# Zero rows under the remainders of the keys in the first attention of a two-block kernel

## The chip, the cores and the metric

The kernel runs on one core of one Trainium2 chip, as one launch. Its time is the device time of that launch in microseconds, the median of several runs; lower is better. Engines are named as in the profile: PE is TensorE's matmul, PEld its weight load, DVE is VectorE, ACT is ScalarE, POOL is GpSimd, SP issues the DMAs.

## The reference, cut to what matters

The reference takes 256 tokens of width 1024 through a first block (gated branch mixer, cross attention to a memory, mixture of experts) and a second one: an attention with three branches (`nsa_mixer`), an MLP, a differential attention and another MLP, each under a modulation that depends on a condition. What counts here is the attention with three branches: 16 query heads of width 64 in four groups, each group with its own key and value head for a "selected" and a "window" branch.

```
q_rot = apply_partial_rope(rms_norm(q), cos, sin)          # 16 heads x 64
ks    = apply_partial_rope(rms_norm(ks, k_gain[1]), ...)   # 4 groups x 64, selected
kw    = apply_partial_rope(rms_norm(kw, k_gain[2]), ...)   # 4 groups x 64, window
ss = einsum('bghqd,bgqnld->bghqnl', q_rot, ks_selected) / 8   # causal softmax, then times values
sw = einsum('bghqd,bgkd->bghqk',   q_rot, kw_window)   / 8    # causal softmax, then times values
out = gate0 * o_cmp + gate1 * o_sel + gate2 * o_win
```

With 256 tokens there are four blocks of 64 keys and the four best are selected, so both branches see all earlier keys: the scores of a query are the products with two key sets under one causal mask.

## The kernel before, in words

A scheduler sets the order of the instructions of each engine before the run, from the program and a simulated timeline; on the chip each engine takes its instructions in that fixed order and waits on semaphores.

[...] To keep the precision, an operand is kept as two tiles: its rounded value (hi) and the remainder (lo). For the scores, `qrT` holds the rotated queries of a head with the hi part in rows 0 to 63 and the lo part in rows 64 to 127, [128, 256 tokens] a head. `kTd` holds the hi part of the keys twice over the rows, so that one product over 128 rows gives (hi + lo of q) times hi of k. `kTl` holds the lo part of the keys in 64 rows only; a second product, over the 64 rows of the queries' hi part, adds hi of q times lo of k to the same PSUM bank. A third product of the identity (`identb`) with the causal mask `cmask` adds the mask.

`kv_block(s, c0)` makes keys and values of one branch s: a projection, the norm of the heads, the rotation, transposes on TensorE, then `kTd` by ScalarE (line 1189) and `kTl` by VectorE (line 1190). The layout is [rows, group, token tile, branch, 128 keys], so one product takes both branches of a token tile.

`att(p_, t)` does two heads (pair `p_`) and one tile of 128 queries (`t`). For t = 0 a product has 256 columns, for t = 1 it has 512. Line 1393 holds the products with `kTd` and `kTl`, line 1396 those with the mask. VectorE takes the maximum (lines 1400 and 1401), ScalarE the exponential with its sum (line 1411), VectorE divides and gates (1413 to 1417). Two rounds later TensorE transposes the probabilities (line 1428), ScalarE or VectorE copies them out (1434, 1432), and a round later TensorE multiplies with the values (line 1444) and adds the compressed branch (line 1446). `skewed` runs 16 such generators (eight pairs, two tiles each) as a software pipeline, one new one each round. Between rounds, `fill` puts modulation products: `ada_step` loads 512 KB of `w_ada` into one of two buffers (line 427) and multiplies it with the condition (line 432, eight products with 32 columns of stationary each).

The score products take four PSUM banks in turn, two for each `att`.

On GpSimd, `rescale` multiplies the residual stream `xT` with gains (line 1136) and with a norm (line 1137) near 534 to 557 us; the tiles `Sc` are cleared at line 1350 for the compressed branch.

Of the kernel before, what the change touches and what calls it, by code (L numbers as in the profile page):

```python
# [11 lines left out]
F32 = mybir.dt.float32  # L12
F32R = mybir.dt.float32r
# [3 lines left out]
OP = mybir.AluOpType  # L17
# [21 lines left out]
def two_blocks_kernel(ctx, tc, A, out):  # L39
# [10 lines left out]
    # PSUM's eight banks, shared out anew for each phase: outputs of long runs of matmuls (mm), what hangs  # L50
    # on a chain of other engines (ax), long accumulations (acc), modulation rows (ada)
# [24 lines left out]
    # ---------------------------------------------------------------- helpers  # L76
# [6 lines left out]
    def behind(e, ins):  # L83
        """ins is issued behind the fence of its engine (an order for the scheduler, no wait)"""
        if e in fence:
            tc.add_manual_dep(ins.ins, fence[e].ins.name, NOSYNC, reason="behind the norm")
        return ins
# [17 lines left out]
    class wmat:  # L105
        """the hi and lo parts of w2d[:, c0:c0+cols], as [128, cols] pairs, one for each 128 rows"""
# [30 lines left out]
    def mm_fm(ps, w, x, xk, c, first, last, ncol=P, **kw):  # L137
        """ps[ncol features, tokens] += w[:, c:c+ncol]^T x[:, xk, :]"""
        (whi, wlo), (xh, xl) = w, x
        T.matmul(ps, whi[:, c:c + ncol], xh[:, xk, :], start=first, stop=False, **kw)  # L140
        T.matmul(ps, whi[:, c:c + ncol], xl[:, xk, :], start=False, stop=False, **kw)  # L141
        return T.matmul(ps, wlo[:, c:c + ncol], xh[:, xk, :], start=False, stop=last, **kw)  # L142

    def mm_tm(ps, xT, xk, t0, w, first, last):
        """ps[128 tokens, cols] += x[:, xk, t0:t0+128]^T w"""
# [5 lines left out]
    def fm_block(w2d, K, c0, x, w=None, first=False):  # L151
        """256 output features: a bank [128, 2, tokens]; first: x is still under way"""
        w = w.load() if w else wmat(w2d, K, c0, 256)
        ps = bank("fm")
        if first:
            # one group for the bank: its first product clears both halves
# [11 lines left out]
    def tm_steps(w2d, c0, xT, emit, cols=512, w=None):  # L168
        """512 output columns for both token tiles, a tile at a time"""
# [19 lines left out]
    def later(gen):  # L189
        """gen's first step now, its other steps one at a time behind the next blocks of matmuls"""  # L190
# [12 lines left out]
    def skewed(gens, fill=None):  # L203
        """software pipeline: each round starts a generator and moves the others on by one step, newest first"""
# [13 lines left out]
    def log_exp():  # L218
        """ScalarE's table with both Ln and Exp, for what follows"""
# [5 lines left out]
    def inv_rms(ss, n, scale, tag, pool=None):  # L225
        """1/sqrt(ss * scale + EPS) for ss [128, n], with one Newton step on top of the tables' exp(-ln / 2)"""
# [5 lines left out]
    def newton(ss, y, h, t, scale, add=EPS, p=P):  # L232
        """y = 1/sqrt(ss * scale + add)"""
# [7 lines left out]
    def norm_rows(x, dst):  # L241
        """dst = x / rms(x), for x [128 tokens, 1024]"""
# [20 lines left out]
    def rstd(ss, add=EPS):  # L263
        """1/rms of the tokens from their sums of squares on all partitions"""
# [4 lines left out]
    class norm:  # L269
        """the norm of x times gA plus gB, as hi and lo"""  # L270
# [6 lines left out]
        def squares(self, c):  # L277
            """features 256c on of x: their squares' sums over partitions; those of the first 768 are added up before"""
# [39 lines left out]
    def resid(c, ps, gate=None, nx=None):  # L318
        """features 256c on: x += gate * ps, and what the next norm takes from them"""
# [11 lines left out]
    def to_fm(h, aT, t, g):  # L331
        """rows [128 tokens, 1024] times gains to hi/lo feature-major columns of token tile t"""
# [12 lines left out]
    def out_first(aT, w, k1, k0=0, ps=None):  # L345
        """the first block of out_proj up to row block k1, for an input that is still under way"""
# [7 lines left out]
    def out_proj(aT, w2d, nx, gate=None, ws=(), ps0=None):  # L354
        """x += gate * (a @ w)"""
# [9 lines left out]
    # ---------------------------------------------------------------- constants  # L365
# [10 lines left out]
    # the residual stream, feature-major  # L376
# [7 lines left out]
    # causal mask of a diagonal block, twice  # L384
# [6 lines left out]
    # ---------------------------------------------------------------- adaLN rows  # L391
# [3 lines left out]
    def cols(n, name, *parts):  # L395
        """vectors as columns: rows of 128 values turned, [128, n]"""
# [14 lines left out]
    # a part of a layer's modulation row at a time, 1024 columns, in steps of 128 rows of w_ada: on TensorE, 256 for  # L411
    # each of its four column tiles, or summed up over steps on VectorE
# [22 lines left out]
    def ada_mm(n=1, pool=None):  # L435
        """steps on TensorE, or with a pool for the sum on VectorE"""
# [47 lines left out]
    def adaln(i, j, g):  # L484
        """columns of (1 + scale) * g and shift of sublayer j"""
# [10 lines left out]
    # ================================================================ block 1  # L496
    with tc.tile_pool(name="kv", bufs=1, reuse_waits="tile") as kvp:
# [15 lines left out]
        # ---- gated branch mixer  # L513
        win = A["w_in"][0]
        log_exp()
        with tc.tile_pool(name="mix", bufs=1, reuse_waits="tile") as mx:
# [17 lines left out]
            def turned(src, name, c):  # L534
                """features 256c on of two tiles of rows, feature-major"""
# [18 lines left out]
            # the memory's norm, for its keys and values  # L554
# [10 lines left out]
            # rope tables, [128 tokens, tile, 8]  # L565
# [48 lines left out]
            # conv branch  # L614
# [30 lines left out]
            # gated short conv branch  # L645
# [20 lines left out]
            # pool branch  # L666
# [20 lines left out]
            # layer norm over the conv channels  # L687
# [29 lines left out]
            # gates 1 and 2 with their branches  # L717
# [43 lines left out]
        # ---- cross attention  # L761
        phase(mm=3, ax=3, ss=1)
        with tc.tile_pool(name="xa", bufs=2, reuse_waits="tile") as xp, tc.tile_pool(name="ad", bufs=B_X, reuse_waits="tile") as ad:
# [68 lines left out]
            # logits, feature-major, then turned  # L832
# [11 lines left out]
    # ---- hierarchical mixture of experts  # L844
# [7 lines left out]
    def head_rstd(pool, src, n, dim, tag):  # L852
        """1/rms over the last axis of src [128, n, dim]"""
# [6 lines left out]
    def head_norm(pool, dst, src, n, gain, tag):  # L860
        """dst [128, n, 64] = rms_norm(src) * gain, for src in PSUM"""
# [4 lines left out]
    def rope(pool, dst, src, t, n):  # L866
        """the first 16 of 64 columns of dst [128, n, 64] rotated; dst may be src"""
# [11 lines left out]
    with (tc.tile_pool(name="ad3", bufs=5, reuse_waits="tile") as ad,  # L879
# [18 lines left out]
        def first_max(l, nm):  # L898
            """max over the last axis, and the one-hot of its first place"""
# [11 lines left out]
        # ranks within the groups  # L911
# [21 lines left out]
        # the tokens' rows, for the gather  # L933
# [16 lines left out]
        def gating():  # L950
            """o1: each token's weights of the experts of its group"""
# [35 lines left out]
        # the first weights, in tiles of their own  # L987
# [5 lines left out]
        def moe_pass(slot, okm, nx=None, pre=()):  # L993
            """experts on the tokens whose slot is set, 128 slots to a group"""
# [102 lines left out]
        # tokens past a group's 128 slots: a pass of their own, before the others'  # L1097
# [9 lines left out]
        # block 1 ends in x r1 g_f with r1 = 1/sqrt(mean(x^2) + EPS); the mean square of that and its EPS over  # L1107
        # r1^2 are mean(x^2 (g_f^2 + EPS)) + EPS^2, so that block 2 starts on x g_f over the root of that
# [31 lines left out]
    # ================================================================ block 2  # L1140
    # ---- NSA
# [9 lines left out]
    with ExitStack() as st2:  # L1151
# [4 lines left out]
        if True:  # L1156
# [6 lines left out]
            # keys twice over the rows, and what their rounding leaves  # L1163
            kTd = npl.tile([P, 4, 2, 2, P], F32R, name="kTd")
            kTl = npl.tile([64, 4, 2, 2, P], F32R, name="kTl")
            vTM = npl.tile([P, 2, 2, 4, 64], F32, name="vTM")
            qT = act.tile([P, 8, S], F32, tag="aTl", name="qT")
            # rotated queries, a head's hi over its lo
# [5 lines left out]
            # selected and window keys and values  # L1174
            def kv_block(s, c0):
                def emit_k(t, ps):
# [13 lines left out]
                    V.tensor_tensor(kTl[:, :, t, s, :], z[0:64], kTd[0:64, :, t, s, :].bitcast(F32), op=OP.subtract)  # L1190
# [3 lines left out]
            # queries  # L1194
# [22 lines left out]
            def gate_block():  # L1217
                """sigmoid of the gates' logits: feature-major products, then turned"""
# [14 lines left out]
            # compressed keys and values: token-pair columns of four groups, then the position embeddings  # L1233
            if True:
# [23 lines left out]
                def compress():  # L1258
# [27 lines left out]
                    # keys: [64 (group, n), 64]  # L1286
# [21 lines left out]
                    # values: [(4 copies, 32 n), group, 64]  # L1308
# [26 lines left out]
            # compressed branch: probabilities times gate, transposed to [(4 heads, 32 n), tile of heads, q]  # L1335
# [366 lines left out]
```

## Time and profile before

| | us |
|---|---|
| median of 3 timed runs | 1259.2 |
| lowest and highest of them | 1256.54, 1259.34 |
| profiled execution: span from first to last instruction | 1263.1 |
| PE busy in the span | 1214.8 |
| DVE busy | 891.7 |
| ACT busy | 695.9 |
| POOL busy | 26.0 |

The page of the profile gives no other time for the profiled execution than its span. The score products of line 1393 run from 629.6 to 694 us; there are 32 with `kTd` and 32 with `kTl`. PEclk, where it is shown, is the clock that TensorE was granted, as a share of 2.4 GHz: 1.00 is 2.4 GHz, 0.50 is 1.2 GHz. Starts of matmuls are recorded, their ends are modelled, so the distance from one start to the next says more than a duration. A matmul is written with its rows and stationary columns (64\*128) and the output (64x512 is 64 rows of moving data with 512 columns).

### The profile page before, as it was taken

Reading aid. Unit: us, or ns where it says so; the run is one execution under the profiler, and the core shown is the slowest. Engines: PE = TensorE matmul, PEld = TensorE weight load, DVE = VectorE, ACT = ScalarE, POOL = GpSimd, SP = SyncE. Lnnn points to the kernel's source line nnn. Section 1 sums busy time; section 2 is a strip of 40 time slices with the busy share of each in tenths; the row PEclk is TensorE's granted clock in tenths of the full one; section 3 lists DMA queues with packets and bytes.
Section 4 is the critical chain, followed back from the end, with each engine's and each line's share of the span. In section 5 each row is a group of like instructions: output and inputs, shape, how many; then the busy total and the mean of one; then the engine's idle time right before and its main releaser. Section 6 shows DMA issues by size and latency. Waiting matters only on the chain.

```text
span 1263.1 us, 22514 instructions
## 1 busy us (share of the span) xinstructions
PE 1214.8 (96%) x8762; PEld 1079.8 (85%) x8762; DVE 891.7 (71%) x1672; ACT 695.9 (55%) x1163; POOL 26.0 (2%) x33
## 2 busy tenths in 40 slices
PE   7999999999879999899999989999999999999998
PEld 6989999989667888688656879999988767999998
DVE  7999967564568999696756685486679766645453
ACT  6644447453357777566346465455556554655453
POOL 0000000000000000060000000000000000000000
PEclk8999999999889999999769999999999999999999
DMA  7565565791267999665431697586746445555551
GB/s 247 190 220 174 159 205 186 269 305 37 97 219 259 347 354 345 231 205 169 149 110 58 213 345 267 192 302 221 281 167 207 130 134 201 196 196 179 194 172 34
DMA packets 177551, 257.76 MB, mean 204 GB/s; under 512 B 14239, under 2 KB 138999, under 8 KB 177436
## 3 DMA queue, kind: packets, MB, share of 16 engines
q1 hardware_dynamic: 177436, 256.24, 61.1%
q8 instruction: 71, 1.16, 0.4%
q14 instruction: 44, 0.36, 0.1%
HBM read 255.15 MB, written 1.05 MB: 203 GB/s over the span
## 4 chain that ended last, share of the span: by engine, by line
PE 65%; DVE 3%; DMA 2%; ACT 1%; issue 1%; ACTq 0%; DVEq 0%
PE fm L141 6%; PE fm L142 6%; PE fm L140 6%; PE mo L140 5%; PE mo L141 5%; PE mo L142 5%; PE tm L147 3%; PE tm L149 3%; PE tm L148 3%; PE gu L149 2%; PE gu L147 2%; PE gu L148 2%; PE s L1393 2%; PE ada L432 1%; PE py L148 1%; PE py L149 1%
## 5 line engine op out<-in xcount | busy, mean ns | idle before, releaser
L99 DVE TENSOR_TENSOR wlo<-raw,whi 128x1024 fp32r<-128x1024 f32 (+1 forms) x382 | 456.8, 1218 | 178.0 <-ACT whi L98 173.9
L98 ACT ACTIVATE whi<-raw 128x1024 fp32r<-128x1024 f32 (+1 forms) x382 | 391.6, 1048 | 275.4 <-PE fm L141 149.3
L141 PE MATMUL fm<-hTl,whi 128*128 128x256 f32 (+1 forms) x968 | 276.7, 286 | 5.6 <-DVE hTl L216 3.9
L140 PE MATMUL fm<-hTh,whi 128*128 128x256 f32 (+1 forms) x968 | 276.3, 286 | 3.2 <-ACT hTh L215 3.2
L142 PE MATMUL fm<-hTh,wlo 128*128 128x256 f32 (+1 forms) x968 | 275.0, 284 | 0.0
L141 PEld LDWEIGHTS fm<-hTl,whi 128*128 128x128 f32 (+1 forms) x968 | 185.8, 192 | 7.7 <-DVE hTl L216 5.8
L140 PEld LDWEIGHTS fm<-hTh,whi 128*128 128x128 f32 (+1 forms) x968 | 185.8, 192 | 5.7 <-ACT hTh L215 4.6
L142 PEld LDWEIGHTS fm<-hTh,wlo 128*128 128x128 f32 (+1 forms) x968 | 185.7, 192 | 0.2
L141 PE MATMUL mo<-ul,whi 128*128 128x256 f32 x512 | 142.8, 280 | 0.0
L142 PE MATMUL mo<-uh,wlo 128*128 128x256 f32 x512 | 142.7, 280 | 0.0
L140 PE MATMUL mo<-uh,whi 128*128 128x256 f32 x512 | 141.7, 281 | 0.0
L141 PEld LDWEIGHTS mo<-ul,whi 128*128 128x128 f32 x512 | 96.3, 188 | 0.0
L142 PEld LDWEIGHTS mo<-uh,wlo 128*128 128x128 f32 x512 | 96.2, 188 | 0.0
L140 PEld LDWEIGHTS mo<-uh,whi 128*128 128x128 f32 x512 | 95.5, 188 | 0.4 <-issue 0.4
L147 PE MATMUL tm<-whi,hTh 128*128 128x512 f32 x176 | 69.4, 400 | 0.7 <-ACT hTh L215 0.7
L148 PE MATMUL tm<-wlo,hTh 128*128 128x512 f32 x176 | 68.9, 393 | 0.0
L149 PE MATMUL tm<-whi,hTl 128*128 128x512 f32 x176 | 68.1, 392 | 0.0
L141 PE MATMUL fm<-oTl,whi 128*128 128x256 f32 x192 | 55.0, 289 | 0.9 <-DVE oTl L1613 0.8
L140 PE MATMUL fm<-oTh,whi 128*128 128x256 f32 x192 | 53.9, 288 | 1.4 <-ACT oTh L1612 1.3
L142 PE MATMUL fm<-oTh,wlo 128*128 128x256 f32 x192 | 53.6, 283 | 0.0
L147 PE MATMUL gu<-whi,xgh 128*128 128x512 f32 x128 | 51.1, 401 | 1.8 <-ACT xgh L1011 1.8
L627 DVE SCALAR_TENSOR_TENSOR acv<-apad,chv,acv 128x256 f32<-128x256 f32 x120 | 51.3, 475 | 0.0
(522 smaller groups left out, 2163.1 us busy)
## 6 DMA issues: line engine op xcount, KB each, us to landing
ada<-in_w_ada_dram SPq DMA_DIRECT2D x96, 512.0 KB, 4.7
raw<-in_w_mlp_in_dram SPq DMA_DIRECT2D x64, 512.0 KB, 3.8
raw<-in_w_mlp_out_dram SPq DMA_DIRECT2D x64, 512.0 KB, 5.1
raw<-in_w_in_dram SPq DMA_DIRECT2D x48, 512.0 KB, 3.8
raw<-in_w_e_down_dram SPq DMA_DIRECT2D x32, 512.0 KB, 5.2
raw<-in_w_e_gate_dram SPq DMA_DIRECT2D x61, 256.0 KB, 5.0
raw<-in_w_e_up_dram SPq DMA_DIRECT2D x61, 256.0 KB
raw<-in_diff_w_in_dram SPq DMA_DIRECT2D x24, 512.0 KB, 4.1
```

What stands on the lines that cost most here:

```text
L98: behind("A", SC.activation(hi[:, :n], raw[:, :n], AF.Copy))
L99: last["lo"] = behind("V", V.tensor_tensor(lo[:, :n], raw[:, :n], hi[:, :n].bitcast(F32), op=OP.subtract))
L140: T.matmul(ps, whi[:, c:c + ncol], xh[:, xk, :], start=first, stop=False, **kw)
L141: T.matmul(ps, whi[:, c:c + ncol], xl[:, xk, :], start=False, stop=False, **kw)
L142: return T.matmul(ps, wlo[:, c:c + ncol], xh[:, xk, :], start=False, stop=last, **kw)
L147: T.matmul(ps, xh[:, xk, t0:t0 + P], w[0], start=first, stop=False)
L148: T.matmul(ps, xh[:, xk, t0:t0 + P], w[1], start=False, stop=False)
L149: return T.matmul(ps, xl[:, xk, t0:t0 + P], w[0], start=False, stop=last)
L432: behind("T", T.matmul(ada_part["ps"][32 * j:32 * j + 32, :], w, r[:, S * j:S * j + S], start=start, stop=stop, skip_group_check=True))
L627: V.scalar_tensor_tensor(acv[:, f, :], apad[:, f, j:j + S], chv[:, f, j:j + 1], acv[:, f, :], op0=OP.mult, op1=OP.add)
L1393: T.matmul(ss[hp][:, :n], u, k[:, gi, 0:t + 1].rearrange("p a s q -> p (a s q)"), start=k is kTd, stop=False)
```

## The change

`kTl` gets 128 rows instead of 64. GpSimd fills rows 64 to 127 with zeros once, VectorE writes rows 0 to 63 as before, and the second product of the scores takes all 128 rows of the queries (hi over lo) with it; the lo part of the queries meets zeros. The rest of the difference is comments that are gone; one line is added, so that lines from 1166 on have a number higher by one.

```
             kTd = npl.tile([P, 4, 2, 2, P], F32R, name="kTd")
-            kTl = npl.tile([64, 4, 2, 2, P], F32R, name="kTl")
+            kTl = npl.tile([P, 4, 2, 2, P], F32R, name="kTl")
+            G.memset(kTl[64:128].bitcast(F32), 0.0)
...
-                    V.tensor_tensor(kTl[:, :, t, s, :], z[0:64], kTd[0:64, :, t, s, :].bitcast(F32), op=OP.subtract)
+                    V.tensor_tensor(kTl[0:64, :, t, s, :], z[0:64], kTd[0:64, :, t, s, :].bitcast(F32), op=OP.subtract)
...
                     q = qrT[:, 2 * p_ + hp, t * P:(t + 1) * P]
-                    for u, k in ((q, kTd), (q[0:64], kTl)):
-                        T.matmul(ss[hp][:, :n], u, k[:, gi, 0:t + 1].rearrange("p a s q -> p (a s q)"), start=k is kTd,
+                    for k in (kTd, kTl):
+                        T.matmul(ss[hp][:, :n], q, k[:, gi, 0:t + 1].rearrange("p a s q -> p (a s q)"), start=k is kTd,
                                  stop=False)
```

On GpSimd, the order before, from the rescaling of `xT` to the end (`al` and `Sc` are tiles of the compressed branch, `nr` the norm):

```order
L1136 TENSOR_SCALAR xT<-xT,gcols 128x256 x2
L1340 IOTA al 128x16 x2
L1136 TENSOR_SCALAR xT<-xT,gcols 128x256 x6
L1137 TENSOR_TENSOR xT<-xT,nr 128x256 x8
L1350 MEMSET Sc 128x512 x2
```

and the same place of the changed kernel:

```order
L1136 TENSOR_SCALAR xT<-xT,gcols 128x256 x2
L1341 IOTA al 128x16 x2
L1136 TENSOR_SCALAR xT<-xT,gcols 128x256 x2
L1166 MEMSET kTl 64x2048
L1136 TENSOR_SCALAR xT<-xT,gcols 128x256 x4
L1137 TENSOR_TENSOR xT<-xT,nr 128x256 x8
L1351 MEMSET Sc 128x512 x2
```

The memset of `kTl` stands in the middle of the products with the gains, ahead of twelve instructions of the rescaling and the two memsets of `Sc`.

On TensorE, one tile of 256 columns and one of 512 in the middle of the attention, in the changed kernel (`s_` is a bank of scores, `pz` a bank for transposes; the order writes the output's rows):

```order
L1394 MATMUL s_8730<-kTd,qrT 128x256
L1394 MATMUL s_8730<-kTl,qrT 128x256
L1397 LDWEIGHTS identb
L1397 MATMUL s_8730<-cmask,identb 128x256
L1394 MATMUL s_8770<-kTd,qrT 128x512
L1394 MATMUL s_8770<-kTl,qrT 128x512
L1397 LDWEIGHTS identb
L1397 MATMUL s_8770<-cmask,identb 128x256
L1429 MATMUL pz<-ident,E_8678 128x128
```

Nothing moved here: apart from the numbers of lines and tiles the rows are those of before, and so is the whole order of TensorE, VectorE, ScalarE and SP.

## Rows read from the trace of the kernel before

**Rows 1.** Windows: stretch, its us, then busy us (instructions) of each engine, PEclk, DMA

```profile
643.60:657.80 14.20, 14.20 (x65) 8.61 (x61) 5.50 (x19) 5.30 (x22) 0.00 (x0) 0.51 0.33 104
...
666.80:675.00 8.20, 8.20 (x69) 5.06 (x69) 6.35 (x24) 4.94 (x22) 0.00 (x0) 1.00 0.21 69
...
682.70:689.80 7.10, 7.10 (x54) 4.84 (x53) 5.36 (x20) 4.18 (x17) 0.00 (x0) 1.00 0.00 0
```

**Rows 2.** Chain of waits from 636 to 697 us, shares by engine and line

```profile
by line: PE s L1393 33.5%; PE o L1444 19.1%; PE pz L1428 18.1%; PE s L1396 10.0%; PE ada L432 9.4%; PE o L1446 9.1%; PE ax L470 1.1%; PE fm L140 0.5%
```

**Rows 3.** Chain of waits, 615 to 637 us: start, us, what

```profile
630.38 0.61 PE ada L432 x8
...
631.01 4.12 DMA ada<-in_w_ada_dram
```

**Rows 4.** Timeline of PE, two trios at full clock: start us, us, line, operands, shape

```profile
661.69 0.48 PE L1393 MATMUL s<-kTd,qrT 128*128 128x512 f32 x1
662.10 0.49 PE L1393 MATMUL s<-kTl,qrT 64*128 64x512 f32 x1
662.52 0.28 PE L1396 MATMUL s<-cmask,identb 128*128 128x256 bf16 x1
...
668.01 0.36 PE L1393 MATMUL s<-kTd,qrT 128*128 128x256 f32 x1
668.30 0.38 PE L1393 MATMUL s<-kTl,qrT 64*128 64x256 f32 x1
668.61 0.28 PE L1396 MATMUL s<-cmask,identb 128*128 128x256 bf16 x1
```

**Rows 5.** Chain of waits elsewhere, single products: 512 columns at half and full clock, 256

```profile
364.33 0.43 PE gu L147
...
607.11 0.23 PE tm L147
...
708.96 0.12 PE fm L141
```

**Rows 6.** Timeline of PE, pairs of score products at full clock

```profile
630.88 0.73 PE L1393 MATMUL s<-kTd,qrT 128*128 128x512 f32 x2
631.54 0.50 PE L1393 MATMUL s<-kTl,qrT 64*128 64x256 f32 x2
631.97 0.39 PE L1396 MATMUL s<-cmask,identb 128*128 128x256 bf16 x2
```

**Rows 7.** Timeline of PE, a trio at half clock

```profile
637.20 0.80 PE L1393 MATMUL s<-kTd,qrT 128*128 128x512 f32 x1
637.93 0.79 PE L1393 MATMUL s<-kTl,qrT 64*128 64x512 f32 x1
638.65 0.40 PE L1396 MATMUL s<-cmask,identb 128*128 128x256 bf16 x1
```

**Rows 8.** Line 1393 in three stretches: count, duration ns min/median/max, starts, shapes

```profile
L1393 PE MATMUL s<-kTl,qrT x2: 380/381/382, 636.1 to 636.7; 64*128 64x256 f32 x2
...
L1393 PE MATMUL s<-kTl,qrT x6: 576/792/793, 637.9 to 651.7; 64*128 64x512 f32 x4, 64*128 64x256 f32 x2
...
L1393 PEld LDWEIGHTS s<-kTd,qrT x20: 186/190/201, 658.2 to 693.3; 128*128 128x128 f32 x20
...
L1393 PEld LDWEIGHTS s<-kTl,qrT x20: 182/183/183, 658.5 to 693.7; 64*128 64x128 f32 x20
L1393 PE MATMUL s<-kTl,qrT x20: 380/436/502, 658.5 to 693.7; 64*128 64x256 f32 x10, 64*128 64x512 f32 x10
```

**Rows 9.** Timeline of POOL near 598 us

```profile
598.03 0.52 POOL L1350 MEMSET Sc<- 128x512 f32 x1 [40.66 <-PE ax L1212]
```

**Rows 10.** Timeline of PE, two modulation steps

```profile
663.17 0.64 PE L432 MATMUL ada<-ada,cond 128*32 128x256 f32 x8
...
668.82 0.64 PE L432 MATMUL ada<-ada,cond 128*32 128x256 f32 x8
```

**Rows 11.** Windows, between the fall and the rise of the clock

```profile
637.25:657.60 20.35, 20.35 (x89) 11.56 (x88) 10.66 (x42) 9.53 (x40) 0.00 (x0) 0.50 0.29 92
```

## What the change will do to the time: the prediction

> **What bounds the kernel now.** I read the page first: TensorE is the busiest engine, and line 1393, the two products of the scores, is the only line of this change in the chain of work that ended last. Then I cut the span into stretches and looked at the one where these products run, 627 to 697 us. TensorE is busy from end to end there, VectorE less [rows 1]. The chain of waits from 636 to 697 us is made of TensorE work alone, and a third of it is line 1393 [rows 2]. So between 636 and 697 us time taken from TensorE is time taken from the kernel, until another engine is late. Ahead of 635.2 us it is not: there the chain runs through a DMA of 4.12 us that was issued behind the modulation products at 630.38 us, ahead of the first second score products, so what these save ends in a wait for it [rows 3].
>
> The reader is to look next at start times, not at durations. In a trio of kTd, kTl and mask at the full clock, each of the two steps around kTl takes 0.41 and 0.42 us with 512 columns, 0.29 and 0.31 us with 256 [rows 4]. Elsewhere, products on 128 rows that each load another stationary tile stand 0.23 us apart with 512 columns and 0.12 us with 256 [rows 5]. So about 0.18 us is lost on the way into the 64-row product and as much on the way out. It is not the 64-row product itself. Where two kTd, two kTl and two masks stand in pairs, the two kTd take 0.66 us up to the first kTl, that is 2 x 0.23 and one loss of 0.2; the two kTl of 256 columns take 0.43 us up to the mask, 2 x 0.12 and one loss of 0.19 [rows 6]. Between equals nothing is lost; each loss stands where the row count changes.
>
> **The change part by part.** The second product has the same columns, the same count and the same place, but its stationary queries and its moving keys now have 128 rows. Both changes of row count around it go; nothing is added to TensorE, since the number of columns stays.
>
> Price of one kTl at the full clock: (0.41 - 0.23) + (0.42 - 0.23) = 0.37 us with 512 columns; (0.29 - 0.12) + (0.31 - 0.12) = 0.36 us with 256. I take 0.37. At the lower clock: the steps are 0.73 and 0.72 us with 512 columns [rows 7], against 0.43 us between equals [rows 5], so 0.59 us; four of the six products there have 512 columns and I take 0.59 for all.
>
> Counts: two at the full clock before the clock falls, six at the lower clock, twenty at the full clock after it has risen [rows 8]; the other four of 32 are the pairs ahead of the DMA wait and count nothing. The sum for TensorE is 22 x 0.37 + 6 x 0.59 = 8.1 + 3.5 = 11.6 us.
>
> What is late next: an iteration of one pair of heads (two query tiles, four kTl) takes 7.1 us at 682.7 us, and would take 7.1 - 4 x 0.37 = 5.6; VectorE is busy 5.36 us of it and 6.35 of 8.2 us at 666.8 us [rows 1]. Its instructions stand in a fixed order and each waits for TensorE or ScalarE, so I do not believe that it runs without a gap: I let it keep half a microsecond of waiting in each iteration, which gives 5.36 + 0.5 = 5.9 instead of 5.6 us and 6.35 + 0.5 = 6.85 instead of 8.2 - 1.5 = 6.7 us. That is 0.3 us in each of the last two iterations and 0.15 in one more, the other two having more room: 0.8 us taken back, an estimate. At the lower clock VectorE has 5.50 us in 14.20 and takes back nothing [rows 1].
>
> The memset of 64 rows of 2048 zeros is new on GpSimd. The nearest row is a memset of 512 columns in 0.52 us [rows 9], so 2.1 us if it goes by columns, 0.5 us if it is a fixed cost. It stands in the middle of the rescaling of xT, and what is queued behind it (four products with the gains, eight with the norm, then the memsets of Sc) waits for it, and for the release of the space it writes. GpSimd sits idle 40.66 us before the memset of Sc [rows 9], which covers both; I count nothing. If it took VectorE's turn at memory for its whole length it would cost 2.1 us, if that wait outlasted the idle time, more; below nothing it cannot go, as it removes no work. No wait is added to a product: the kTl products carry the wait they had.
>
> The modulation products between the scores need a DMA each, and there are two buffers. The one that feeds 668.82 us can be issued when the products of 663.17 us are through; the one in the chain took 4.12 us [rows 3, 10]. The gap of 5.65 us shrinks by two kTl to 4.9 us, and the products and the landing need 0.64 + 4.12 = 4.8 us of it: just room enough, and a late landing costs tenths.
>
> So 11.6 - 0.8 = 10.8 us, on the profiled span of 1263.1 us: 1252.3 us. The median of the timed runs is 1259.2 us, 3.9 us under that span, and the page gives no other time for the profiled execution, so I take the difference to the median: 1248.4 us. What follows the stage (the loads of the next weights, which are issued when its space is free) moves forward with it.
>
> Against this stands a rule. The trace: the loads of kTd take 190 ns and those of kTl 183 ns, nearly the same [rows 8]. The Trainium skill, "TensorE: Matmul & The Clock Gate", section "LDWEIGHTS (loading the stationary operand)", says that a load costs by its columns and not by its rows, and the section "Part 3: Packing small matmuls — row/col tiling" that a load runs under a product in flight only when their row groups differ. By the first, 128 rows cost no more than 64, and the trace agrees. By the second, a second product on the same rows would still have its load in the open. In this trace the opposite holds: equal rows hide the load [rows 5, 6], and the time would stay at 1259 us only if kTl behaved otherwise than its neighbours.
>
> **The rivals.**
>
> A. The sum above: 1248.4 us, with 1247.5 to 1251 us as its own range (11.6 us if VectorE keeps up, 8.4 us if it takes back four times what I give it). Chance 0.45.
>
> B. The clock rises earlier. In the stretch from 637.25 to 657.60 us it is granted at half [rows 11], after the wait for the DMA that ended at 635.13 us [rows 3]; it came back during a stretch in which no kTl ran. Without the losses at the row changes TensorE has fewer gaps in that stretch, and the clock may return in it sooner; no row here shows whether it does. A comparable iteration takes 14.2 us at half and 7.1 at full [rows 1], so each microsecond at half that becomes full gives back half of itself. Of the 20.4 us, 16.9 are left; if a quarter to all of them turn full, that is 2 to 8 us more: 1240 to 1246.5 us. Against it: the idle time ahead of the fall gets longer, since the DMA wait takes what the pairs save. Chance 0.27.
>
> C. VectorE and ScalarE become the bound of the last five iterations, by latency more than by busy time: reduce, exponential, scaling and transposes follow each other across engines. If the twenty kTl there bring a third of 7.4 us, the sum is 0.7 + 3.5 + 2.5 = 6.7 us: 1252.5 us; if nothing, 4.2: 1255 us. For it: 5.36 us busy of the 5.6 us left; against it: the chain now shows no piece of VectorE's in this stretch [rows 2]. Chance 0.13.
>
> D. The load of the second product stays in the open, as the rule above would have it, or the loss comes from something else than the row count. Time 1258 to 1260 us. The pairs [rows 6] speak against it. Chance 0.09.
>
> E. Slower: the clock stays at half to the end of the stage. With shorter products TensorE waits more often for VectorE between 657 and 697 us, and such gaps were what stood ahead of the fall at 637 us. The 39 us there, 31.6 after the change, would take 31.6 us longer at half; the whole gain of 10.8 us is gone when 11 us of that work runs at half. At the full price: 1259.2 - 10.8 + 31.6 = 1280 us; with half of it 1264 us. Against it: TensorE has no wait in that stretch now [rows 2], and VectorE's load leaves gaps of tenths. Chance 0.06.
>
> **How the numbers follow.** The likeliest case gives 1248.4 us. The range takes in A, most of B and nearly all of C: 1242 to 1255 us; outside are the deep end of B (0.07), D and E. A measurement of this kernel tells about 0.3%, 3.8 us, from no change, so faster means below 1255.4 us: A, B and nearly all of C, 0.84. Within: D and the tail of C, 0.10. Slower: E, 0.06.
>
> **What would show it.** The kTl products in the trace after have 128 rows, and the steps kTd to kTl and kTl to mask are 0.23 us (512 columns) and 0.12 us (256) at the full clock. The iterations from 657 to 697 us take 5.6 to 6.9 us, and VectorE's share in them rises to nine tenths. The DMA wait at 635 us grows by about 0.8 us. GpSimd has one more memset near 540 us and still waits for TensorE before Sc. B shows as a stretch at half clock under 15 us, E as a second one after 657 us. The prediction is wrong if the steps stay at 0.41 us (then the row count was not the cause), or if they fall and waits for VectorE or ScalarE of more than 4 us stand in TensorE's rows instead.

## The result, and the profile after

| | before | after |
|---|---|---|
| median of 9 timed runs, us | 1260.19 | 1252.14 |
| lowest to highest, us | 1256.54 to 1268.81 | 1244.65 to 1254.12 |
| span of the profiled execution, us | 1263.1 | 1250.3 |

The ratio after to before is 0.9918, 95% interval 0.9889 to 0.9947: faster by 0.8%, between 0.5 and 1.1%. The medians lie 8.05 us apart; their ratio alone is 0.9936, inside the interval. The runs of both scatter with the clock that TensorE was granted, and those of before scatter further up.

The first thing to look at in the profile after is line 1393, now 1394, alone. All 32 products with `kTl` have 128 rows, and their loads take as long as those of 64 rows took [rows 8]: 191 ns against 183. The columns are count, shortest, median and longest duration in ns, first and last start, shapes.

```profile
L1394 PEld LDWEIGHTS s<-kTl,qrT x32: 188/191/192, 632.3 to 678.7; 128*128 128x128 f32 x32
L1394 PE MATMUL s<-kTl,qrT x32: 278/380/476, 632.5 to 679.0; 128*128 128x256 f32 x16, 128*128 128x512 f32 x16
```

Two trios (kTd, kTl, mask) with 512 columns at the full clock in the timeline of TensorE after, which answer to [rows 4]:

```profile
671.77 0.48 PE L1394 MATMUL s<-kTd,qrT 128*128 128x512 f32 x1
672.09 0.40 PE L1394 MATMUL s<-kTl,qrT 128*128 128x512 f32 x1
672.33 0.28 PE L1397 MATMUL s<-cmask,identb 128*128 128x256 bf16 x1
672.37 0.47 PE L1394 MATMUL s<-kTd,qrT 128*128 128x512 f32 x1
672.68 0.40 PE L1394 MATMUL s<-kTl,qrT 128*128 128x512 f32 x1
672.92 0.29 PE L1397 MATMUL s<-cmask,identb 128*128 128x256 bf16 x1
```

The step from kTl to the mask fell from 0.42 to 0.24 us, what [rows 5] led one to expect. The step from kTd to kTl fell only from 0.41 to 0.32. But look where the second kTd starts: 0.04 us behind the start of a mask that has 256 columns to move. It seems that its recorded start lies too early, and that the step behind it looks longer for that, before the change as after it. The first kTd, behind transposes, has the same 0.32 us, so it is not the mask alone. The distance from trio to trio does not depend on this: it is 0.60 us here.

For the whole stage I take one stretch, from the first products with the values (line 1444) to the first product of the output projection; 22 of the 32 second products lie in it. In three further traces of the kernel before that had the full clock in it, it took 44.78 us each time; in three traces of the kernel after 38.04, 38.04 and 38.05 us. The windows of one trace each (stretch, its us, then busy us and instructions of PE, PEld, DVE, ACT, POOL, then PEclk, DMA share, GB/s), before:

```profile
642.05:686.83 44.78, 44.78 (x350) 28.53 (x349) 31.20 (x116) 27.40 (x111) 0.00 (x0) 1.00 0.23 74
```

and after, with the two last whole iterations, which answer to [rows 1]:

```profile
663.82:670.17 6.35, 6.35 (x62) 4.42 (x60) 5.48 (x21) 5.31 (x22) 0.00 (x0) 1.00 0.29 86
670.17:676.01 5.84, 5.84 (x53) 4.48 (x52) 4.91 (x19) 3.92 (x18) 0.00 (x0) 1.00 0.00 0
643.82:681.86 38.04, 38.04 (x350) 26.76 (x349) 30.89 (x117) 27.21 (x111) 0.00 (x0) 1.00 0.28 84
```

TensorE is busy throughout in both. So 6.74 us went, 0.306 us for each of the 22 products, and nothing came in their place. The chain of waits over the same stretch says which lines lost it, before:

```profile
by line: PE s L1393 31.3%; PE o L1444 22.4%; PE pz L1428 18.2%; PE o L1446 11.1%; PE s L1396 9.2%; PE ada L432 7.6%; PE ax L470 0.5%
```

and after:

```profile
by line: PE o L1445 26.4%; PE s L1394 24.2%; PE pz L1429 20.0%; PE o L1447 12.9%; PE ada L432 9.0%; PE s L1397 7.0%; PE ax L470 0.6%
```

Line 1393 goes from 31.3% of 44.78 us, 14.0, to 24.2% of 38.04, 9.2; the masks from 4.1 to 2.7 us. Together that is 6.3 of the 6.74 us. The masks were never touched: the chain, it seems, goes by the modelled ends of products, and so books part of the way out of the 64 rows on them. The starts say it more plainly. The order of the products in the stretch is the same in both traces, so each step from one start to the next has its partner. The 22 steps that begin at a kTd fell from 8.04 to 5.68 us, the 22 that begin at a kTl from 8.27 to 4.08, those that begin at a mask from 2.66 to 2.62, and the steps of no other group by more than 0.15 us. So the way out of the 64 rows gave 0.19 us for each of the 22. The way in gave 0.09 us for 19 of them, and 0.20 us for the three whose kTd itself stands right behind a kTl.

### The profile page after: what moved, and what is told of

Its sections match the earlier page's. It is cut to its first block, busy times and chain, and to the rows that moved or that the text cites. A ratio compares the mean times of both kernels' runs of the same rounds, so it can differ in the third digit from the quotient of the medians.

```text
span 1250.3 us, 22518 instructions
## 1 busy us (share of the span) xinstructions
PE 1200.8 (96%) x8762; PEld 1076.0 (86%) x8762; DVE 889.7 (71%) x1672; ACT 695.6 (56%) x1163; POOL 26.6 (2%) x34
## 3 DMA queue, kind: packets, MB, share of 16 engines
q8 instruction: 71, 1.16, 0.4%
## 4 chain that ended last, share of the span: by engine, by line
PE 64%; DMA 3%; DVE 3%; ACT 1%; issue 1%; ACTq 0%; DVEq 0%
PE fm L141 6%; PE fm L140 6%; PE fm L142 6%; PE mo L140 5%; PE mo L141 5%; PE mo L142 5%; PE tm L147 3%; PE tm L149 3%; PE tm L148 3%; PE gu L149 2%; PE gu L147 2%; PE gu L148 2%; DMA ada<-in_w_ada_dram 2%; PE ada L432 1%; PE py L148 1%; PE py L149 1%
```

## The experiments

**Is it the rows of the product, or the tile and its zeros?** `e1_zeros_only` keeps the 128-row tile and the memset and multiplies 64 rows:

```
-                    for k in (kTd, kTl):
-                        T.matmul(ss[hp][:, :n], q, k[:, gi, 0:t + 1]...
+                    for u, k in ((q, kTd), (q[0:64], kTl[0:64])):
+                        T.matmul(ss[hp][:, :n], u, k[:, gi, 0:t + 1]...
```

> Undoes one half of the change: kTl keeps its 128 rows and the memset of zeros, but the second product reads only 64 rows of it and of the queries, as before. Theory T: the time of before, ratio 0.998 to 1.002, steps of 0.41 and 0.42 us around the 512-column kTl at the full clock. Rival M (the gain comes from another place: the space that kTl takes, or the order that the scheduler finds with the memset): the time of after, ratio 0.990 to 0.994. A cost of the memset by itself (2 us if VectorE were held up for it) would show as 1.0015.

Ratio to before 1.0007 (0.9981 to 1.0032). The timeline of its TensorE has the old steps back, 0.41 and 0.43 us:

```profile
684.91 0.48 PE L1394 MATMUL s<-kTd,qrT 128*128 128x512 f32 x1
685.32 0.50 PE L1394 MATMUL s<-kTl,qrT 64*128 64x512 f32 x1
685.75 0.28 PE L1397 MATMUL s<-cmask,identb 128*128 128x256 bf16 x1
```

The tile, its memset and the order that comes with them gain and cost nothing that can be measured.

**Is it the 64-row product, or the change of row count?** Two kernels in which the order is tied, so that each pair of heads does both kTd, both kTl, both masks; one with 64 rows (`e3_pairs`), one with 128 (`e3b_pairs128`), the same otherwise:

```
+                ks = []
+                for rows, k in ((P, kTd), (64, kTl)):
+                    for hp in range(2):
+                        i = T.matmul(ss[hp][:, :n], qrT[0:rows, 2 * p_ + hp, ...], k[...], start=k is kTd, stop=False)
+                        if k is kTl and hp == 0:
+                            tc.add_manual_dep(i.ins, ks[1].ins.name, NOSYNC, reason="pairs")
+                        ks.append(i)
...
+                    tc.add_manual_dep(i.ins, ks[3].ins.name, NOSYNC, reason="pairs")
```

> The second product stays on 64 rows, but the order is tied so that the products of both heads with kTd come first, then both with kTl, then both masks: one change of row count into a pair of kTl and one out of it, in place of two for each kTl. Theory T (the loss is at the change of row count): half the gain of after on the 28 products that stood alone, 14 x 0.29 = 4 us and up to 6 with the products at half clock, ratio 0.995 to 0.997. Rival S (the 64-row product is slow by itself, wherever it stands): no gain, ratio 0.999 to 1.002; two kTl side by side would then stand 0.3 to 0.4 us apart in the trace and not 0.12 to 0.23. The new order may cost something on its own account; the next kernel has the same order and tells that.

> The same tied order with the second product on 128 rows. Against the kernel with pairs on 64 rows it has 32 changes of row count less (one in and one out of each of 16 pairs). Theory T: faster than the 64-row pairs by half the gain, 14 to 16 pairs x 0.29 = 4 to 5 us, and about equal to after if the order costs nothing (ratio 0.990 to 0.994). Rival S: faster than the 64-row pairs by the whole gain, 8 us or more. If the order costs, both kernels with pairs are late by the same amount.

Ratios to before: 0.9993 (0.9966 to 1.0020) and 0.9947 (0.9928 to 0.9966). The stretch from the first products with the values to the output projection took 46.48 and 43.11 us at the full clock. So between 64 and 128 rows lie 3.37 us for the 11 pairs in it. Of these, 0.39 us is a wait of TensorE for a DMA that was shorter with 128 rows (0.73 and 0.34 us, its only idle time in the stretch); the products themselves give 2.98 us, 0.27 us a pair. That is about what a single product gave, 0.306 us, though a pair has two. It is the change of row count that costs, in and out together about 0.3 us, and not the product. The two timelines side by side, first 64 rows:

```profile
673.67 0.50 PE L1393 MATMUL s<-kTd,qrT 128*128 128x512 f32 x1
674.10 0.73 PE L1393 MATMUL s<-kTl,qrT 64*128 64x512 f32 x2
674.76 0.39 PE L1399 MATMUL s<-cmask,identb 128*128 128x256 bf16 x2
675.09 1.09 PE L1448 MATMUL o<-PT,vTM 128*64 128x128 f32 x14
```

then 128:

```profile
672.38 0.50 PE L1394 MATMUL s<-kTd,qrT 128*128 128x512 f32 x1
672.71 0.62 PE L1394 MATMUL s<-kTl,qrT 128*128 128x512 f32 x2
673.18 0.39 PE L1400 MATMUL s<-cmask,identb 128*128 128x256 bf16 x2
673.50 1.09 PE L1449 MATMUL o<-PT,vTM 128*64 128x128 f32 x14
```

From kTd to the products with the values it is 1.42 us against 1.12. On whole runs the two lie 5.2 us apart by median, near the 4 to 5 us of theory T. The tied order itself is bad: with 128 rows the stretch takes 5.07 us more than that of after, and the cause of that stays open. That ate what the pairs with 64 rows won, and I had not foreseen its size: half of the gain was expected for that kernel and almost none came.

**What is left of the second product?** `e2_no_second` is before without it:

```
-                    for u, k in ((q, kTd), (q[0:64], kTl)):
...
+                    T.matmul(ss[hp][:, :n], q, kTd[:, gi, 0:t + 1].rearrange("p a s q -> p (a s q)"), start=True,
+                             stop=False)
```

> Leaves out the second product of the scores (hi of the queries times the remainder of the keys), so the scores are less exact; kTl is still made. Theory T: what is left of the second product after the change is its columns, 0.12 us (256) and 0.23 us (512), 32 x 0.175 = 5.6 us; so this kernel is 5 to 6 us faster than after, 1246 us, ratio 0.988 to 0.991. Rival V (after the change VectorE and ScalarE set the pace of the last five iterations, 5.4 of 5.9 us busy): less is left to win, 2 to 4 us against after, ratio 0.991 to 0.993, and TensorE shows waits for VectorE or ScalarE in the attention.

Ratio 0.9923 (0.9887 to 0.9960). That is the number of rival V, but the ratios of after itself lie on both sides of it (0.9918 to 0.9939): on whole runs no gain over after can be seen, though the interval takes in theory T as well. The stretch took 36.96 us, 1.08 us under that of after, but it does not hold the same work: in this order 24 products with the values and two with the compressed branch, of two passes each, fall behind its end. Up to the last product of the compressed branch, which takes in all of them, this kernel needs 50.42 us (from 641.91 us on) and after 48.15 us (from 643.82 us on), with 428 products against 444 of all kinds. So it is 2.27 us slower there with 16 products less, which speaks against theory T. TensorE is idle 1.36 us in that time, against 0.23 after. Of this 0.97 us lies in the stretch, which the waits account for only with what follows them (the columns: waits in us, times, longest):

```profile
PE fm L140 <- ACT E L1410: 0.4, 1, 0.4
PE pz L1427 <- DVE E L1416: 0.4, 1, 0.4
PE o L1443 <- DVE oTl L216: 0.2, 1, 0.2
```

and the scheduler put the modulation products into other places, in pieces of two and four. How much of the loss is waiting and how much order stays open, and so does what the columns of the second product cost. What the run does show is that TensorE begins to wait for VectorE and ScalarE when its own work in this stage gets shorter still.

**Does the same hold for the other product on 64 rows?** The compressed branch multiplies its values with 64 rows of probabilities, at line 1446. `e4_vc128` adds, to after, a second tile for the values with the other 64 rows zero:

```
-            Vc = npl.tile([P, 4, P], F32, name="Vc")
+            Vcs = [npl.tile([P, 4, P], F32, name="Vc"), nt("Vc2").rearrange("p a (b c) -> p (a b) c", b=2)]
...
-                T.matmul(o_, Vc[b0:b0 + 64, gi, :], PcT[b0:b0 + 64, gi, t * P:(t + 1) * P], ...
+                T.matmul(o_, Vcs[p_ % 2][:, gi, :], PcT[:, gi, t * P:(t + 1) * P], ...
```

> On top of the change, the same for the other product of this stage on 64 rows: the compressed branch's values (16 products, each in two passes) get a second tile whose other 64 rows are zeros, so that this product takes all 128 rows of the probabilities. Theory T: row change in and out goes, 0.1 to 0.3 us for each of 16, 2 to 4 us faster than after, ratio to before 0.989 to 0.992. Rival K (the loss there belongs to the change in columns, as the products with the values ahead of it have 64 columns of stationary and it has 128): the pair of passes still takes 0.41 us and the time is that of after. VectorE gets one more memset of 512 columns and one tile of a pool shared with the modulation's rows is held through the stage, which may cost up to 1 us.

Ratio 0.9877 (0.9845 to 0.9909). That was more than its trace explained, so it ran again beside after (`e7_after_side`, `e8_vc128_side`), and alone on the kernel before (`e6_vc_only`), with the same edit.

> The changed kernel beside the two below on one chip. From the traces: from the first products with the values to the first product of the output projection the stage takes 38.04 us, against 44.78 us before where both have the full clock throughout, 6.74 us for 22 second products; with 6 more ahead of it, less a DMA wait of 0.7 us that is new, 7.5 us in all. Theory T: ratio 0.993 to 0.995, and 38.0 us again in the trace if the clock is full there.

> The kernel with both products on 128 rows, beside after on the same chip, since the first look gave more than its trace explains: its stage was 1.16 us shorter than that of after, its median 4 us lower. Theory T (only the row changes count): 1 to 2 us faster than after, ratio to before 0.991 to 0.994. Rival O (the tile that is held in the pool shared with the modulation's rows, and the order that comes of it, help in another place): 3 to 5 us faster than after, ratio 0.988 to 0.991.

> The change to the compressed branch's values alone, on the kernel before: the second product of the scores stays on 64 rows. Theory T: the two changes do not touch each other, so this one alone gives what it gave on top: 1 to 2 us, ratio 0.998 to 1.000. Rival O: 3 to 5 us, ratio 0.996 to 0.998.

On one chip: after 0.9928 (0.9904 to 0.9952), just under what was expected, median 1250.56 us; both on 128 rows 0.9907 (0.9882 to 0.9933), 1248.08 us; the second change alone 1.0010 (0.9986 to 1.0034). The stretch took 38.05, 36.88 and 43.62 us. Against 38.05 and 44.78 that is 1.17 and 1.16 us: the two changes add up, and the 1 to 2 us that theory T of the later runs expected hold for the stage. The 2 to 4 us that theory T of `e4_vc128` expected do not. On whole runs 1.2 us is below what these measurements tell: the intervals of after and of both overlap, and the second change alone shows nothing. So outside the stage the runs do not decide between theory T and rival O. Both together is the fastest kernel here by median. The gain a product is smaller, 0.1 us for each of twelve in the stretch, since only its way out got shorter: the way in, from the products with the values, takes 0.59 us with 64 rows and with 128. In the timeline of TensorE of `e4_vc128`, it is 0.24 us from the pair of passes to the next scores:

```profile
642.59 0.66 PE L1446 MATMUL o<-PT,vTM 128*64 128x128 f32 x8
643.18 0.49 PE L1448 MATMUL o<-PcT,Vc 128*128 128x128 f32 x2
643.42 0.48 PE L1395 MATMUL s<-kTd,qrT 128*128 128x512 f32 x1
```

and in that of after 0.41:

```profile
643.82 0.66 PE L1445 MATMUL o<-PT,vTM 128*64 128x128 f32 x8
644.41 0.48 PE L1447 MATMUL o<-PcT,Vc 64*128 64x128 f32 x2
644.82 0.50 PE L1394 MATMUL s<-kTd,qrT 128*128 128x512 f32 x1
```

Where products with 64 stationary columns follow, it stays at 0.42 us (0.41 in after):

```profile
652.70 0.49 PE L1448 MATMUL o<-PcT,Vc 128*128 128x128 f32 x2
653.12 1.09 PE L1446 MATMUL o<-PT,vTM 128*64 128x128 f32 x16
```

So rival K holds for the way in and for this way out: where the count of stationary columns changes anyway, filling the rows wins nothing.

**What does the clock add?** The changed kernel again, and three more traces of the kernel before:

> The changed kernel once more, to learn how far its time depends on the stretches in which TensorE's clock is granted at half. Theory T (each change of row count beside the second product costs TensorE time, 0.29 us a product at the full clock as trio against trio, 0.5 to 0.6 us at half): 6.4 us from 22 products at the full clock and 3 us from six if they fall into a half stretch, so a ratio to before of 0.992 to 0.994 in runs that have the same half stretches. Rival C (the clock does it: the stretch at half from 637 to 657 us of the kernel before is gone after the change, and that is worth most of the gain): the ratio scatters with the clock, down to 0.988, and the trace after shows no half stretch between 637 and 660 us whenever the time is at its low end.

> The kernel before once more, for its trace alone: the stretch at half clock from 637 to 657 us of its first trace added 6 x (0.59 - 0.37) us to the forecast. Theory P (that stretch is a thing of the single run, and the kernel's typical run, at a mean clock near 0.980, has less of it): the trace shows at most 7 us at half between 630 and 660 us whenever the mean clock is 0.979 or more, and the 28 products outside the pairs then lose 0.29 us each, 8 us in all. Rival C (the stretch belongs to the kernel before, since its gaps at the row changes let the clock fall): 20 us at half again there, at any mean clock.

> As the run above, one more look at the kernel before: with two more traces it can be seen whether the half stretch between 636 and 658 us comes with each of them (rival C) or not (theory P).

> A third look at the kernel before. So far the stretch at half clock from 636 to 658 us came with one of three traces of it (and with that of the kernel with zeros only, which runs in the same order). Theory P (the half stretch varies from run to run): if the stage has the full clock, it takes 44.8 us from the first products with the values to the first product of the output projection, as in the two looks that had it; if it has a half stretch, more by about half of its length.

`e0_after_again`: ratio 0.9939 (0.9915 to 0.9962), as theory T had it, median 1251.08 us. The three executions of before took 1259.62, 1255.32 and 1258.06 us. The time at half clock, from windows, as twice the missing share of PEclk:

| trace | 628 us to the first products with the values | from there to the output projection | length of the latter |
|---|---|---|---|
| before, first trace | 13.0 | 9.8 | 49.08 |
| e1_zeros_only | 12.9 | 9.8 | 49.17 |
| before, three further traces | 6.9, 0.0, 7.0 | 0, 0, 0 | 44.78, 44.78, 44.78 |
| after, three traces | 3.8, 3.4, 1.3 | 0, 0, 0 | 38.04, 38.04, 38.05 |

The long half stretch of [rows 11] came in two of five traces with the old products (and not in that of `e6_vc_only`, which has them too: 0.8 and 0 us), so theory P is right: it is no fixed part of the kernel before. In none of three traces after was there more than 3.8 us. Over all runs whose clock is on record, the mean clock gives a median of 55.2 us at half for before (55 runs) and 45.0 for after (21 runs). That points the way of rival B, less time at half after the change, but no experiment held the clock or the waits ahead of it fixed, so this stays a difference that was seen, not a cause that was shown. To set it aside, I take the runs with a mean clock of 0.980 to 0.983 alone: 1259.0 us for before (mean of 23), 1251.0 for after (mean of 13). At the same clock the change is worth 8.0 us.

## Why the prediction was right, by its steps

The forecast was 1248.4 us, 10.8 us below the median then known, in a range of 1242 to 1255 us. The ratio of 0.9918 lies in case A; the medians measured lie 8.05 us apart, which from 1259.2 us leads to 1251.15 us, the upper edge of A. The mechanism was right. Its terms were not all the right size, and that the sum came no further out is in part luck, since one error went against the others. The time alone would not tell A from rival C (1252.5 us); the traces do.

- **What bounds the stage**: right. In the stretch TensorE was busy 44.78 of 44.78 us and is busy 38.04 of 38.04. From 627 us on, in the trace that the prediction read, it was busy 68.74 of 70.00 us and not quite from end to end; the rest is the DMA wait that the prediction itself names.
- **The loss sits at the change of row count**: right; the pairs show it directly. Rival D is out: the load of a kTl with 128 rows is no longer in the open. In the timelines of the weight loads (PEld) the 64-row load, in the second further trace of before, starts together with its product at 675.40 us; the 128-row load starts 0.24 us ahead of its product at 672.09 us, under the kTd:

```profile
675.40 0.18 PEld L1393 LDWEIGHTS s<-kTl,qrT 64*128 64x128 f32 x1 [0.25 <-issue]
```

```profile
671.85 0.19 PEld L1394 LDWEIGHTS s<-kTl,qrT 128*128 128x128 f32 x1
```

  So loads on the same rows are hidden here, those across a change of rows are not. With that the rule of the Trainium skill, "TensorE: Matmul & The Clock Gate", section "Part 3: Packing small matmuls — row/col tiling", is out for this case as I read it, that only loads on other row groups are hidden; I had left out that the same section also lets a load go ahead into a background weight buffer. "TensorEngine Tiling (Array Packing)" of the Trainium skill, section "Key Properties", says that changing the tiling mode drains TensorE; the trace shows a price of such a change, 0.306 us for the way in and out of 64 rows, but not whether a drain or the load in the open makes it up.
- **The price of a product at the full clock**: 0.37 us predicted, 0.306 measured. This is the step that failed most plainly. I put 0.18 us on the way in and as much on the way out. The way out was right, 0.19 us; the way in gave 0.09 us for 19 of the 22. I had subtracted a step between equals (0.23 us) from one that begins at a kTd behind a product of another kind, and the 0.09 us by which such a step is longer are still there after the change (0.32 us). The pairs [rows 6] have the same error: the 0.66 us from two kTd to the first kTl fell to 0.57 and not to 0.46. Trio to trio would have come closer: in one of the further traces of before, 0.88 us from kTd to kTd with 512 columns, 0.60 us after. That row, in the timeline of TensorE of the second further trace:

```profile
674.99 0.48 PE L1393 MATMUL s<-kTd,qrT 128*128 128x512 f32 x1
675.40 0.50 PE L1393 MATMUL s<-kTl,qrT 64*128 64x512 f32 x1
675.83 0.28 PE L1396 MATMUL s<-cmask,identb 128*128 128x256 bf16 x1
675.87 0.47 PE L1393 MATMUL s<-kTd,qrT 128*128 128x512 f32 x1
```

- **The six products at half clock**: 3.5 us predicted, 0.82 found. They are at half only in runs like the one I read. At the full clock six times 0.306 would be 1.8 us. From the modulation products that end the first wait to the first products with the values it took 8.48 us in the second further trace of before and 7.66 us after, both at the full clock: TensorE's busy time fell by 1.39 us, from 8.21 to 6.82, and its idle time rose from 0.27 to 0.84, most of it a DMA wait that was new (next point). The price at half was too high as well, for the same reason as the one at full. `e0_after_again` has a trio in a stretch that was granted half:

```profile
633.97 0.78 PE L1394 MATMUL s<-kTd,qrT 128*128 128x512 f32 x1
634.54 0.63 PE L1394 MATMUL s<-kTl,qrT 128*128 128x512 f32 x1
634.97 0.44 PE L1397 MATMUL s<-cmask,identb 128*128 128x256 bf16 x1
```

  Its steps of 0.57 and 0.43 us, in place of 0.73 and 0.72 [rows 7], make 0.45 us where 0.59 was priced.
- **The modulation's DMAs**: I looked at the pair near 668 us and found room. The wait came earlier in the stage, where two loads follow each other closely. Timeline of TensorE after, in brackets the idle time ahead and its releaser:

```profile
636.16 0.64 PE L432 MATMUL ada<-ada,cond 128*32 128x256 f32 x8 [1.72 <-DMA ada<-in_w_ada_dram]
...
640.09 0.64 PE L432 MATMUL ada<-ada,cond 128*32 128x256 f32 x8
641.45 0.64 PE L432 MATMUL ada<-ada,cond 128*32 128x256 f32 x8 [0.73 <-DMA ada<-in_w_ada_dram]
```

  The first wait was 1.26 us in the first trace of before and is 1.72 us here. But it was 1.73, 0.77 and 1.65 us in the three further traces of before, and 1.82 and 1.19 us in the two others of after: that it grew by the 0.8 us of the forecast is not shown. The second wait stands in none of the four traces of before. After has it in two of three, with 0.73 and 0.42 us; in the one without it, that of `e0_after_again`, part of the way there ran at half. That fits a stage that comes to these products earlier than their load.
- **VectorE takes back 0.8 us**: it took back nothing. In the two iterations above it is busy 5.48 of 6.35 and 4.91 of 5.84 us, nine tenths were expected; TensorE has no wait for it or for ScalarE in the stretch. The last iteration came to 5.84 us where 5.6 stood in the forecast, only because the price was smaller. Rivals C and E did not occur. The sign of B, a half stretch of under 15 us, did come (3.8 us at half in the first trace of after), but traces of before show as little, so it does not speak for B.
- **The memset**: 1.85 us where 2.1 were reckoned, in the middle of the rescaling, and GpSimd still idles 42.18 us ahead of Sc [rows 9]. Timeline of POOL after:

```profile
539.28 1.85 POOL L1166 MEMSET kTl<- 64x2048 f32 x1
541.22 8.00 POOL L1136 TENSOR_SCALAR xT<-xT,gcols 128x256 f32<-128x256 f32 x4
549.19 8.10 POOL L1137 TENSOR_TENSOR xT<-xT,nr 128x256 f32<-128x256 f32 x8
599.47 0.53 POOL L1351 MEMSET Sc<- 128x512 f32 x1 [42.18 <-PE ax L1213]
```

Put together from the traces: 6.74 us in the stretch and 0.82 us ahead of it (one trace of each kernel), 7.6 us; 8.0 us by the runs at equal clock. The forecast's 10.8 was 1.4 us too much in the price of 22 products (0.064 each), 2.7 us too much in the six at half (3.5 in place of 0.82), and 0.8 us too little for VectorE: 10.8 - 1.4 - 2.7 + 0.8 = 7.5 us.

## What to carry to other kernels

Where a product on fewer rows stands between products on all rows and TensorE is the bound, filling its rows with zeros takes away the changes of row count and, here, cost no time; it gave 0.31 us for each product that stood alone. It gave nothing on a side where the count of stationary columns changed as well. Read the price of such a step over a whole period, from one instruction to the next of its kind, and not from two neighbouring starts. And look at more than one trace before a clock stretch goes into a sum: this one came in two of six.

## What the runs showed that I had not expected

The stretch of the attention repeats to 0.01 us between runs and chips when the clock is full, 44.78 us three times and 38.04 to 38.05 three times, while whole runs scatter by 10 us and more. What a change does inside a stage can be read from a few traces far more finely than from the run times. Tying the order into pairs, which halves the changes of row count, cost 5.07 us in that stretch, more than the 3.4 us that 11 changes saved are worth.
